# Moving input-panel products ahead of five mixer steps in a hybrid decoder layer: five numbers in a hand-written TensorE order

## The chip, the cores and the metric

The kernel runs on one core of one Trainium2 chip. The metric is the device time of one execution in microseconds (us); the shown time is the median of three runs. Five engines work side by side, each through its own list of instructions: TensorE (PE in the profile, with PEld for its weight loads), VectorE (DVE), ScalarE (ACT), GpSimd (POOL) and SyncE (SP), which here issues the loads. An instruction that needs another engine's result waits at the head of its engine's list, and everything behind it on that engine waits too.

## The reference, cut to what matters

One layer over 256 tokens of width 2048, all in float32. The layer normalizes `x`, multiplies it with `w_in`, feeds one half of the result to a causal pooling mixer and the other to an RWKV-7 time mixer with 16 heads of 64, multiplies both outputs with `w_out`, and goes on with a squared-ReLU MLP and a gated embedding.

```python
h = rms_norm(x, attn_norm[i])
z = h @ w_in[0]
z_pool = z[..., :POOL_WIDTH]
zs = token_shift(z[..., POOL_WIDTH:IN_WIDTH], mu_shift[i])
pool_out = ...            # windowed means of z_pool, times pool_w, times pool_scale
# rwkv7_time_mix of zs = [r, k, v, w, a, g], per head and step t:
#   w, a, g come from narrow inputs through small matrices (low rank)
#   kk = k * k_k, normalized;  k = k * (1 + (a - 1) * k_a)
sa = einsum('bhij,bhj->bhi', S, a_t)
S = S * w_t + sa * b_t + v_t * k_t
y = einsum('bhij,bhj->bhi', S, r_t)
# y is normalized per head;  y += sum(r * k * r_k) * v   (the bonus);  y *= g
mix = concatenate([pool_out, rwkv_out])
x = x + mix @ w_out[i]
x = x + square(relu(rms_norm(x) @ w_ffn_up[i])) @ w_ffn_down[i]
x = x + sigmoid(rms_norm(x) @ w_ple_gate[i]) * (p[i] @ w_ple_proj[i])
return rms_norm(x, final_norm)
```

## The kernel before

**Panels.** A weight matrix is loaded in panels of 128 x 1024 (`raw_...`, 512 KB each, issued by SP). Each panel is split for exactness into a high part `wh` (two copies on ACT, L167) and a rest `wl` (one subtraction on DVE, L168). A panel holds two contraction blocks of 128 rows for 512 columns, and there are two tiles of 128 tokens; PE multiplies each block and token tile with the high part twice (the activations' high part at L241, their rest at L242) and then with the rest once (L238). So a panel is eight products with `wh`, taken in four yields of two, and four with `wl`, taken in four yields of one. Three buffers each hold `raw`, `wh` and `wl`, so panel number i takes the buffers of panel i-3: its `raw` is free when the `wl` of that panel is computed, its `wh` and `wl` when PE has multiplied with them. SP issues the loads in order, so a load that waits for its buffer holds up those behind it.

**The queue.** The panel products of the mixer are generators that stand in a list `queue`: `zk0`, `zr0`, `zv0` (key, receptance and value inputs of heads 0 to 7), `zk1`, `zr1` (heads 8 to 15), `zp0` (pooling), `zv1`, `zp1`, and then the output products `o0a` to `o3a`. PE's order is written out by hand: ahead of a mixer step stands a call that takes products out of the queue. `steps(n)` takes n yields, `fill(us)` takes yields until their declared costs (0.45 for two products with `wh`, 0.23 for one with `wl`) reach the number, and `finish(gen)` takes all that is left up to the end of one generator. A larger number moves panel products ahead of a step; the queue is then shorter later on, and the shift ends at the next `finish`. `z_product` ends with `finish`, `fill(us)` and the transposes `zkT`, `zrT` or `zvT` of its result (L498).

**The other engines.** Each yield also advances `pace`, which puts DVE steps of the triangular inverse (`X`, L724 and L728) in between. Up to the end of the low-rank step `wag_out` the orders of DVE and ACT are fixed as written; behind it a scheduler orders DVE and ACT by priority, and it sees the new order of PE too.

**The steps that are touched.**
- *Head and low-rank transposes.* `head` ends with four sums of squares (`sbank`, L441) and `steps(1)`. ACT takes their root (`rs_n`, L450), DVE the reciprocal (L451), ACT scales the low-rank result (`wagS`, two halves, L459), and PE transposes it (`wagT`, L464 and L465).
- *Second key transposes.* ACT scales the finished banks of `zk1` (`zk1s`, L488); PE transposes (`zkT`); ACT and DVE mix each token with its predecessor (`zk_t`, L335 and L336); ACT squares it (`tF_t`, L585); PE sums the squares per head (`kkn`, L595).
- *Bonus sums.* `rwkv_values` multiplies the values (`vt`) and forms the bonus sums (`bsum`, L523) in the two banks that the receptance transposes `zrT` held until DVE read them (L336).
- *State steps.* `rwkv_core` goes over four chunks c of 64 tokens: ACT copies the right-hand side (`R`, L818), PE multiplies (`um`, L854), ACT copies (`UV`, L858), PE forms the state update (`sm`, L863). The values are due in this form for the first eight heads (gi = 0) and the second (gi = 1).

Of the kernel before, what the change touches and what calls it, by code (L numbers as in the profile page):

```python
# [40 lines left out]
def trunk(  # L41
# [32 lines left out]
    def rw_bank(name):  # L74
        return psr.tile([128, 512], F32, tag="rw", name=name)
# [192 lines left out]
    def fill(us):  # L268

        while us > 0 and queue:  # L270
            us -= advance()

    def steps(n):
        for _ in range(n):
            advance()
# [126 lines left out]
    def head():  # L402
        load_xT(0, 1)
        load_wag("tE", 0, 1)
        load_xT(1, 1)
        load_wag("tF", 1, 1)
        ready(8)
        wag_prod(0, 1)
        wag_prod(1, 1)
        steps(8)  # L410
        load_xT(2, 2)
        load_wag("zr", 2, 2)
        load_xT(4, 4)
        load_wag("zv", 4, 2)
        wag_prod(2, 2)
        wag_prod(4, 2)
        steps(8)
        sums.append(squares(0))
        load_wag("BK", 6, 2)
        load_xT(8, 4)  # L420
        load_wag("BKt", 8, 2)
        wag_prod(6, 2)
        wag_prod(8, 2)
        steps(8)
        sums.append(squares(1))
        load_wag("zk", 10, 2)
        load_xT(12, 4)
        load_wag("tE", 12, 2)
        wag_prod(10, 2)
        wag_prod(12, 2)  # L430
        steps(8)
        sums.append(squares(2))
        load_wag("tF", 14, 2)
        wag_prod(14, 2)
        steps(10)
        sums.append(squares(3))
        steps(3)
        derived()
        for tt in range(2):
            for i, q in enumerate((1, 3)):  # L440
                nc.tensor.matmul(  # L441
                    sbank[:, tt : tt + 1], sums[q][:, 0, tt * 128 : (tt + 1) * 128], ones[:, 0:1],
                    start=i == 0 and tt == 0, stop=i == 1, skip_group_check=True,
                )
        steps(1)

    rs1 = const.tile([128, 2], F32, tag="rs", bufs=2, name="rs_n1")

# [324 lines left out]
    def rwkv_values(gi, st, zv):  # L773

        uvs = [rp.tile([128, 2, 8, 64], F32, tag=f"q{i}", name=f"UV{gi}_{i}") for i in range(2)]
        UV = [uvs[c // 2][:, c % 2] for c in range(4)]
        for tt in range(2):
            b = rw_bank("vt")
            for p in range(4):
                nc.tensor.matmul(b[:, p * 128 : (p + 1) * 128], zv[:, p, tt * 128 : (tt + 1) * 128], cen, start=True, stop=True)  # L780
            for i in range(2):
                with tc.high_priority(30000):
                    nc.scalar.activation(flat3(UV[2 * tt + i])[64:128], b[i * 64 : (i + 1) * 64, :], AF.Copy)
        bon = st["rk"]
        bf, vf = flat(bon), flat(zv)
        block_sum(
            st["rk"], f"rk{gi}",
            lambda hf, b: nc.vector.tensor_tensor(
                bf[:, hf * 512 : (hf + 1) * 512], b, vf[:, hf * 512 : (hf + 1) * 512], op=ALU.mult
            ),  # L790
        )
        st["UV"] = UV

    def rwkv_core(gi, st):
# [34 lines left out]
        for c in range(4):  # L829
# [11 lines left out]
            if 0 < c < 3:  # L841
                for e in range(2):
                    r = slice(e * 64, e * 64 + 64)
                    with tc.high_priority(30000):
                        nc.vector.tensor_tensor(
                            nxt[r, :, r], cur[r, :, r], pc[r, :, c : c + 1].to_broadcast([64, 4, 64]), op=ALU.mult
                        )
            fill(1.59 if gi else 1.14)
            ub = rw_bank("um")
            if c < 3:  # L850
                sb = rw_bank("sm")
# [4 lines left out]
                    direct(b_next, c + 1, h)  # L856
            with tc.high_priority(30000):
                nc.scalar.activation(flat3(UV[c])[0:64], ub[0:64, :], AF.Copy)  # L858
            fill(0.72 if gi else 0.86)
            if c < 3:  # L860
                for h in range(8):
                    e, p = h % 2, h // 2
# [33 lines left out]
    def flat3(t_):  # L896
        return t_.rearrange("s h i -> s (h i)")
# [109 lines left out]
    z_zk1 = z_product(4, "zk", "mu_k", 1)  # L1007
# [20 lines left out]
    zv0 = z_zv0()  # L1028
    fill(0.25)
    st1 = rwkv_lora(1)  # L1030
    rwkv_k(1, st1, z_zk1(1.33))
    rwkv_r(1, st1, z_zr1())
    run(beside.pop(0) if beside else ())
    beside.clear()
# [455 lines left out]
```

## Time and profile before

| what | value |
|---|---|
| median of 3 runs | 1180.49 us (1180.44 to 1181.11) |
| the profiled execution | 1180.25 us, its span 1178.2 us |
| granted TensorE clock | 0.998 of full speed |
| DVE, ACT busy | 873.3 us (74%), 709.3 us (60%) |
| HBM | 183 GB/s over the span |

The mixer, in which all five places lie, takes the first part of the span, up to about 345 us; the MLP's products `u_w` and the rest follow. A timeline row gives start, duration, engine, source line, operation and tile names (`out<-in`), the number of instructions in the row, and in brackets the idle time of the engine ahead of it with the releaser. Durations of matmuls overlap, so the distance from one start to the next says how fast PE goes. A table of windows gives the busy time of every engine in a stretch.

### The profile page before, as it was taken

Reading aid. Unit: us, or ns where it says so; the run is one execution under the profiler, and the core shown is the slowest. Engines: PE = TensorE matmul, PEld = TensorE weight load, DVE = VectorE, ACT = ScalarE, POOL = GpSimd, SP = SyncE. Lnnn points to the kernel's source line nnn. Section 1 sums busy time; section 2 is a strip of 40 time slices with the busy share of each in tenths; the row PEclk is TensorE's granted clock in tenths of the full one; section 3 lists DMA queues with packets and bytes.
Section 4 is the critical chain, followed back from the end, with each engine's and each line's share of the span. In section 5 each row is a group of like instructions: output and inputs, shape, how many; then the busy total and the mean of one; then the engine's idle time right before and its main releaser. Section 6 shows DMA issues by size and latency. Waiting matters only on the chain.

```text
span 1178.2 us, 17287 instructions
## 1 busy us (share of the span) xinstructions
PE 1162.5 (99%) x6419; PEld 973.4 (83%) x6419; DVE 873.3 (74%) x1188; ACT 709.3 (60%) x1309; POOL 13.7 (1%) x73
## 2 busy tenths in 40 slices
PE   8999999999999999999999999999999999999997
PEld 8787777788887888888888888888888888888886
DVE  7786996964656666767988987676668879788543
ACT  7776848676545565555665664555556655568543
POOL 2100000000000000000000000000000000000000
PEclk9999999999999999999999999999999999999999
DMA  7464343354465555555556556555555555767511
GB/s 290 154 202 146 135 140 119 119 179 157 160 203 178 177 182 196 184 192 200 187 204 212 198 202 209 186 191 191 185 195 190 202 205 195 290 233 249 197 56 72
DMA packets 60756, 216.81 MB, mean 184 GB/s; under 512 B 6784, under 2 KB 7552, under 8 KB 60288
## 3 DMA queue, kind: packets, MB, share of 16 engines
q1 hardware_dynamic: 60240, 214.99, 52.5%
q8 instruction: 50, 0.82, 0.3%
q10 hardware_dynamic: 432, 0.73, 0.2%
q14 instruction: 34, 0.28, 0.1%
HBM read 213.59 MB, written 2.10 MB: 183 GB/s over the span
## 4 chain that ended last, share of the span: by engine, by line
PE 96%; ACT 1%; DVE 1%; DMA 0%; issue 0%; SPq 0%; POOL 0%; DVEq 0%; POOLq 0%
PE u_w L1112 20%; PE u_w L1117 10%; PE d_b L1231 7%; PE d_b L1229 7%; PE d_b L1230 7%; PE d_w L1231 2%; PE d_w L1229 2%; PE d_w L1230 2%; PE gt_b L242 2%; PE gt_b L241 2%; PE gt_b L238 2%; PE zk_b L241 1%; PE zk_b L242 1%; PE o_b L241 1%; PE o_b L242 1%; PE zv_b L238 1%
## 5 line engine op out<-in xcount | busy, mean ns | idle before, releaser
L1112 PE MATMUL u_w<-h,wh_u 128*128 128x512 f32 x1024 | 321.9, 395 | 0.0
L167 ACT ACTIVATE wh_u<-raw_u 128x512 fp32r<-128x512 f32 x256 | 147.5, 623 | 160.9 <-issue 98.2
L168 DVE TENSOR_TENSOR wl_u<-raw_u,wh_u 128x1024 fp32r<-128x1024 f32 x128 | 156.6, 1224 | 105.2 <-ACT wh_u L167 103.5
L1117 PEld LDWEIGHTS u_w<-h,wl_u 128*128 128x128 f32 x1024 | 192.4, 188 | 45.4
L1117 PE MATMUL u_w<-h,wl_u 128*128 128x256 f32 x1024 | 201.4, 278 | 0.0
L1112 PEld LDWEIGHTS u_w<-h,wh_u 128*128 128x128 f32 x1024 | 156.0, 189 | 0.1
L168 DVE TENSOR_TENSOR wl_gt<-raw_gt,wh_gt 128x1024 fp32r<-128x1024 f32 x24 | 29.4, 1224 | 23.2 <-ACT wh_gt L167 23.2
L167 ACT ACTIVATE wh_gt<-raw_gt 128x512 fp32r<-128x512 f32 x48 | 28.0, 638 | 23.1 <-PE gt_b L242 14.4
L241 PE MATMUL gt_b<-wh_gt,h 128*128 128x512 f32 x96 | 37.3, 389 | 0.0
L242 PE MATMUL gt_b<-wh_gt,h 128*128 128x512 f32 x96 | 37.3, 389 | 0.0
L168 DVE TENSOR_TENSOR wl_o<-raw_o,wh_o 128x1024 fp32r<-128x1024 f32 x16 | 19.6, 1222 | 12.9 <-ACT wh_o L167 9.9
L167 ACT ACTIVATE wh_o<-raw_o 128x512 fp32r<-128x512 f32 x32 | 18.4, 623 | 16.3 <-issue 8.5
L167 ACT ACTIVATE wh_zp<-raw_zp 128x512 fp32r<-128x512 f32 x32 | 18.6, 623 | 15.7 <-PE zp_b L242 7.2
L168 DVE TENSOR_TENSOR wl_zk<-raw_zk,wh_zk 128x1024 fp32r<-128x1024 f32 x16 | 19.4, 1220 | 10.4 <-ACT wh_zk L167 10.4
L241 PE MATMUL zk_b<-wh_zk,hTh 128*128 128x512 f32 x64 | 25.2, 394 | 1.4 <-ACT wh_zk L167 1.4
L241 PE MATMUL zv_b<-wh_zv,hTh 128*128 128x512 f32 x64 | 26.0, 406 | 0.0
L167 ACT ACTIVATE wh_zk<-raw_zk 128x512 fp32r<-128x512 f32 x32 | 18.4, 622 | 12.4 <-PE zv_b L242 4.0
L241 PE MATMUL zp_b<-wh_zp,hTh 128*128 128x512 f32 x64 | 25.7, 401 | 0.0
L238 PE MATMUL gt_b<-wl_gt,h 128*128 128x512 f32 x96 | 25.7, 389 | 0.0
L168 DVE TENSOR_TENSOR wl_zv<-raw_zv,wh_zv 128x1024 fp32r<-128x1024 f32 x16 | 19.4, 1218 | 8.2 <-ACT wh_zv L167 7.4
L241 PE MATMUL zr_b<-wh_zr,hTh 128*128 128x512 f32 x64 | 25.4, 397 | 0.0
L242 PE MATMUL zp_b<-wh_zp,hTl 128*128 128x512 f32 x64 | 25.0, 391 | 0.0
(840 smaller groups left out, 2963.9 us busy)
## 6 DMA issues: line engine op xcount, KB each, us to landing
raw_u<-in_w_ffn_up_dram SPq DMA_DIRECT2D x128, 512.0 KB, 3.5
raw_d<-in_w_ffn_down_dram SPq DMA_DIRECT2D x128, 512.0 KB, 4.3
raw_gt<-in_w_ple_gate_dram SPq DMA_DIRECT2D x24, 512.0 KB, 3.5
raw_zk<-in_w_in_dram SPq DMA_DIRECT2D x16, 512.0 KB, 3.7
raw_zr<-in_w_in_dram SPq DMA_DIRECT2D x16, 512.0 KB, 3.3
raw_zv<-in_w_in_dram SPq DMA_DIRECT2D x16, 512.0 KB, 3.3
raw_zp<-in_w_in_dram SPq DMA_DIRECT2D x16, 512.0 KB, 3.2
raw_o<-in_w_out_dram SPq DMA_DIRECT2D x16, 512.0 KB, 4.2
```

What stands on the lines that cost most here:

```text
L167: nc.scalar.activation(wh[:, a * 512 : (a + 1) * 512], raw[:, a * 512 : (a + 1) * 512], AF.Copy)
L168: nc.vector.tensor_tensor(wl, raw, wh.bitcast(F32), op=ALU.subtract)
L238: nc.tensor.matmul(banks[tt], ah[:, ts_], halves[a][1], start=False, stop=last)
L241: nc.tensor.matmul(banks[tt], ah[:, ts_], halves[a][0], start=i + a == 0, stop=False)
L242: nc.tensor.matmul(banks[tt], al[:, ts_], halves[a][0], start=False, stop=False)
L1112: nc.tensor.matmul(bank[:, ct, :].rearrange("p (s t) -> p s t", s=2), wh[:, cs[ct]], hl, start=k == 0, stop=False, skip_group_check=True,)
L1117: nc.tensor.matmul(bank[:, ct, 0:T], wl[:, cs[ct]], hl[:, 0, :], start=False, stop=k == 15, skip_group_check=True)
L1229: nc.tensor.matmul(banks[n], ah, wh, start=first, stop=False)
L1230: nc.tensor.matmul(banks[n], ah, wl, start=False, stop=False)
L1231: nc.tensor.matmul(banks[n], al, wh, start=False, stop=last)
```

## The change

Five numbers change, and no instruction is added or left out. Ahead of the low-rank transposes six more yields are taken (`steps(7)` for `steps(1)`: two more products with `wl` of panel five of `zk0`, and the eight with `wh` of panel six). Ahead of the second key transposes `fill` rises from 1.33 to 1.90, which is three products. Ahead of the first bonus sums a new `fill(0.92)` takes six products. In the first state step of the first heads the fill ahead of `um` rises from 1.14 to 1.59 and that ahead of `sm` from 0.86 to 1.76, three products each. In `fill(0.00 ...)` nothing is taken. From L784 on, lines of the changed kernel have a number one higher.

```diff
--- before.py
+++ after.py
@@ -442,7 +442,7 @@
                     sbank[:, tt : tt + 1], sums[q][:, 0, tt * 128 : (tt + 1) * 128], ones[:, 0:1],
                     start=i == 0 and tt == 0, stop=i == 1, skip_group_check=True,
                 )
-        steps(1)
+        steps(7)
 
     rs1 = const.tile([128, 2], F32, tag="rs", bufs=2, name="rs_n1")
 
@@ -781,6 +781,7 @@
             for i in range(2):
                 with tc.high_priority(30000):
                     nc.scalar.activation(flat3(UV[2 * tt + i])[64:128], b[i * 64 : (i + 1) * 64, :], AF.Copy)
+        fill(0.00 if gi else 0.92)
         bon = st["rk"]
         bf, vf = flat(bon), flat(zv)
         block_sum(
@@ -845,7 +846,7 @@
                         nc.vector.tensor_tensor(
                             nxt[r, :, r], cur[r, :, r], pc[r, :, c : c + 1].to_broadcast([64, 4, 64]), op=ALU.mult
                         )
-            fill(1.59 if gi else 1.14)
+            fill(1.59 if gi or c == 0 else 1.14)
             ub = rw_bank("um")
             if c < 3:
                 sb = rw_bank("sm")
@@ -856,7 +857,7 @@
                     direct(b_next, c + 1, h)
             with tc.high_priority(30000):
                 nc.scalar.activation(flat3(UV[c])[0:64], ub[0:64, :], AF.Copy)
-            fill(0.72 if gi else 0.86)
+            fill(0.72 if gi else 0.86 if c else 1.76)
             if c < 3:
                 for h in range(8):
                     e, p = h % 2, h // 2
@@ -1028,7 +1029,7 @@
     zv0 = z_zv0()
     fill(0.25)
     st1 = rwkv_lora(1)
-    rwkv_k(1, st1, z_zk1(1.33))
+    rwkv_k(1, st1, z_zk1(1.90))
     rwkv_r(1, st1, z_zr1())
     run(beside.pop(0) if beside else ())
     beside.clear()
```

Since the queue is shared, the orders of ACT and DVE change along with PE's. At the low-rank step, ACT (the rows from the root of the sums on; `wagS` is the scaled low-rank result, `wh_zr` a split receptance panel) has before:

```order
L450 ACTIVATE rs_n_175<-sbank,eps_n 128x2
L459 ACTIVATE wagS<-wag_b_169,rs_n_175 128x288
L459 ACTIVATE wagS<-wag_b_170,rs_n_175 128x288
L335 ACTIVATE zf<-wagT,omu 128x256
L471 ACT_TABLE_LOAD
```

and now:

```order
L450 ACTIVATE rs_n_175<-sbank,eps_n 128x2
L459 ACTIVATE wagS<-wag_b_169,rs_n_175 128x288
L167 ACTIVATE wh_zr_1_622<-raw_zr_1_620 128x512 x2
L459 ACTIVATE wagS<-wag_b_170,rs_n_175 128x288
L335 ACTIVATE zf<-wagT,omu 128x256
```

The split of receptance panel one has moved in between the two halves of `wagS`. At the same place DVE has, before, the last key panel's rest directly ahead of the reciprocal:

```order
L144 TENSOR_SCALAR oka<-par_sb 128x8
L145 SCALAR_TENSOR_TENSOR cen<-jsum,ident 128x128
L168 TENSOR_TENSOR wl_zk_7_561<-raw_zk_7_558,wh_zk_7_560 128x1024
L451 RECIPROCAL rs_n_175<-rs_n_175 128x2
L133 TENSOR_TENSOR wband<-wband,ident 128x128
```

and now:

```order
L168 TENSOR_TENSOR wl_zk_6_518<-raw_zk_6_515,wh_zk_6_517 128x1024
L168 TENSOR_TENSOR wl_zk_7_561<-raw_zk_7_558,wh_zk_7_560 128x1024
L168 TENSOR_TENSOR wl_zr_0_585<-raw_zr_0_582,wh_zr_0_584 128x1024
L451 RECIPROCAL rs_n_175<-rs_n_175 128x2
L133 TENSOR_TENSOR wband<-wband,ident 128x128 x2
```

The rest of receptance panel zero, `wl_zr_0`, has moved ahead of the reciprocal. At the second key transposes, DVE (`zk_t` is the token mix behind `zkT`, `X` the inverse) has before:

```order
L724 TENSOR_TENSOR X_1131<-X_1131,AT_1130 128x120
L728 TENSOR_TENSOR X_1131<-X_1131 128x10x12
L724 TENSOR_TENSOR X_1131<-X_1131,AT_1130 128x121
L336 SCALAR_TENSOR_TENSOR zk_t<-zkT_1350,par_sb,zk_t 128x255
L728 TENSOR_TENSOR X_1131<-X_1131 128x11x11
L336 SCALAR_TENSOR_TENSOR zk_t<-zkT_1351,par_sb,zk_t 128x255
L724 TENSOR_TENSOR X_1131<-X_1131,AT_1130 128x110
L728 TENSOR_TENSOR X_1131<-X_1131 128x11x10
L336 SCALAR_TENSOR_TENSOR zk_t<-zkT_1350,par_sb,zk_t 128x255
L724 TENSOR_TENSOR X_1131<-X_1131,AT_1130 128x108
L336 SCALAR_TENSOR_TENSOR zk_t<-zkT_1351,par_sb,zk_t 128x255
```

and now:

```order
L724 TENSOR_TENSOR X_1131<-X_1131,AT_1130 128x120
L728 TENSOR_TENSOR X_1131<-X_1131 128x10x12
L724 TENSOR_TENSOR X_1131<-X_1131,AT_1130 128x121
L728 TENSOR_TENSOR X_1131<-X_1131 128x11x11
L724 TENSOR_TENSOR X_1131<-X_1131,AT_1130 128x110
L728 TENSOR_TENSOR X_1131<-X_1131 128x11x10
L724 TENSOR_TENSOR X_1131<-X_1131,AT_1130 128x108
L336 SCALAR_TENSOR_TENSOR zk_t<-zkT_1355,par_sb,zk_t 128x255
L336 SCALAR_TENSOR_TENSOR zk_t<-zkT_1356,par_sb,zk_t 128x255
L168 TENSOR_TENSOR wl_zr_3_1446<-raw_zr_3_1443,wh_zr_3_1445 128x1024
L336 SCALAR_TENSOR_TENSOR zk_t<-zkT_1355,par_sb,zk_t 128x255
L336 SCALAR_TENSOR_TENSOR zk_t<-zkT_1356,par_sb,zk_t 128x255
```

Four more steps of the inverse stand ahead of the first `zk_t`, and the rest `wl_zr_3` stands between the second and the third. At the first state step ACT (`wh_zv` is a split value panel, `tmp` belongs to the inverse's use, `UV` follows `um`) has before:

```order
L950 ACTIVATE zt_1942<-zp_b_1585,rs_n_175 128x512
L167 ACTIVATE wh_zv_2_2073<-raw_zv_2_2071 128x512
L818 ACTIVATE R_1966<-rym 64x2x128 x2
L167 ACTIVATE wh_zv_2_2073<-raw_zv_2_2071 128x512
L167 ACTIVATE wh_zv_3_2149<-raw_zv_3_2147 128x512 x2
L710 ACTIVATE tmp_1927<-tmp_1927 64x1024
L858 ACTIVATE UV_0_1655<-um 64x512
```

and now:

```order
L764 ACTIVATE SC_950<-qm 32x8x32 x4
L951 ACTIVATE zt_1929<-zp_b_1585,rs_n_175 128x512
L167 ACTIVATE wh_zv_3_2088<-raw_zv_3_2086 128x512
L819 ACTIVATE R_1981<-rym 64x2x128 x2
L167 ACTIVATE wh_zv_3_2088<-raw_zv_3_2086 128x512
L709 ACTIVATE tmp_1945<-SC_1773 32x1024
L167 ACTIVATE wh_zv_4_2174<-raw_zv_4_2172 128x512 x2
L710 ACTIVATE tmp_1945<-tmp_1945 64x1024
L859 ACTIVATE UV_0_1655<-um 64x512
```

Between `R` and `UV` a piece of `tmp` (L709), which stood ahead of `R` before, has been added; a half panel, a whole panel and L710 stand there in both.

## Prediction

> **What bounds the kernel now.** I read the page first: busy times and the chain that ended last.
>
> ```profile
> span 1178.2 us, 17287 instructions
> PE 1162.5 (99%) x6419; PEld 973.4 (83%) x6419; DVE 873.3 (74%) x1188; ACT 709.3 (60%) x1309; POOL 13.7 (1%) x73
> PE 96%; ACT 1%; DVE 1%; DMA 0%; issue 0%; SPq 0%; POOL 0%; DVEq 0%; POOLq 0%
> ```
>
> PE is the bound: 1162.5 of 1178.2 us busy, 96% of the chain. The change takes no work from PE, so it can win only PE's idle time, 15.7 us at most, and of that only what lies at the five places. The waits of PE, grouped, come next (us, times, longest).
>
> ```profile
> PE bsum L523 <- DVE zr_t L336: 1.0, 1, 1.0
> PE sm L863 <- ACT UV L858: 0.9, 1, 0.9
> PE wagT L464 <- POOL wband L130: 0.8, 1, 0.8
> PE zkT L498 <- ACT zk1s L488: 0.8, 2, 0.6
> PE um L854 <- ACT R L818: 0.4, 1, 0.4
> ```
>
> The five edits stand exactly ahead of these five waits: 1.0 + 0.9 + 0.8 + 0.8 + 0.4 = 3.9 us. But a busy PE need not be a fast one, so I read the windows for what surrounds these waits (busy us and count by engine, granted clock, DMA share, GB/s).
>
> ```profile
> 130.00:160.00 30.00, 28.90 (x142) 22.69 (x140) 29.34 (x57) 21.29 (x41) 0.78 (x3) 1.00 0.52 175
> 250.00:345.00 95.00, 95.00 (x720) 77.81 (x719) 52.93 (x70) 54.27 (x111) 0.96 (x2) 1.00 0.50 169
> ```
>
> From 130 to 160 us DVE is busy 29.34 of 30 us: whatever is put ahead of a DVE step there delays it in full. From 250 to 345 us PE has no idle time, so a lag or a lead gained earlier passes to the end unchanged.
>
> **Edit 1, low-rank transposes.** PE first, then ACT and DVE, around the place.
>
> ```profile
> 36.78 0.48 PE L238 MATMUL zk_b<-wl_zk,hTh 128*128 128x512 f32 x1
> 38.11 0.41 PE L464 MATMUL wagT<-ident,wagS 128*128 128x128 f32 x2 [0.85 <-POOL wband L130]
> 39.95 0.39 PE L242 MATMUL zk_b<-wh_zk,hTl 128*128 128x512 f32 x1
> 41.08 1.07 PE L238 MATMUL zk_b<-wl_zk,hTh 128*128 128x512 f32 x4
> 35.93 1.15 ACT L167 ACTIVATE wh_zr<-raw_zr 128x512 fp32r<-128x512 f32 x2 [0.89 <-PE zk_b L242]
> 37.47 0.89 ACT L459 ACTIVATE wagS<-wag_b,rs_n 128x288 f32<-128x288 f32 x2 [0.23 <-DVE rs_n L451]
> 37.26 0.17 DVE L451 RECIPROCAL rs_n<-rs_n 128x2 f32<-128x2 f32 x1 [0.96 <-ACT rs_n L450]
> 41.74 1.21 DVE L168 TENSOR_TENSOR wl_zr<-raw_zr,wh_zr 128x1024 fp32r<-128x1024 f32 x1
> ```
>
> Five products start from 39.95 to 41.08, 0.227 us each. Ten more ahead of the transposes are 2.3 us; the demand moves from 37.26 to about 39.5, past the 38.11 at which the transposes now start. So far the 0.85 us is gone. But in the new order DVE makes `wl_zr_0` ahead of the reciprocal, and that needs the buffer that PE frees with its last `wl` product of panel five. Two more products behind 36.78 (0.48 long) end at about 37.6; with 1.21 us for `wl_zr_0` the reciprocal starts at 38.9 instead of 37.26, and the first half of `wagS` ends near 39.6. Behind it ACT has `wh_zr_1`, which needs the `wh` buffer of panel six, free when PE ends its eight products, near 39.5; it takes 1.15 us, so the second half ends at about 41.2. The second group of transposes waits for it, and the next product starts near 41.4 where it stood at 41.08 before. I take +0.3 us. The ends: −0.85 (all of the wait goes) and +0.9 (ACT late by half a `wh_zr_1` more). `wl_zr_0` itself was hidden in idle time of DVE; its cover is gone, and the reciprocal pays for it.
>
> **Edit 2, second key transposes.** The two waits of PE, and the ACT step they wait for.
>
> ```profile
> 128.60 0.33 PE L498 MATMUL zkT<-ident,zk1s 128*128 128x128 f32 x1 [0.56 <-ACT zk1s L488]
> 129.18 0.98 PE L498 MATMUL zkT<-ident,zk1s 128*128 128x128 f32 x7 [0.25 <-ACT zk1s L488]
> 127.88 1.24 ACT L488 ACTIVATE zk1s<-zk_b,rs_n 128x512 f32<-128x512 f32 x2
> ```
>
> ACT ends `zk1s` at 129.12, and its order up to there stays. Three more products are 0.68 us, and they fit into the gap of 0.56 + 0.25 = 0.81: I take −0.7, with 0 and −0.8 as ends.
>
> **What follows on edit 2: the head sums `kkn`.** These are eight products behind a fixed fill, and no wait is listed for them. Compare the first group (58.06) with the second (134.64).
>
> ```profile
> 58.06 0.64 PE L595 MATMUL kkn<-tF_t,jhead 128*32 128x256 f32 x8
> 58.63 0.50 PE L241 MATMUL zr_b<-wh_zr,hTh 128*128 128x512 f32 x1
> 134.64 2.13 PE L595 MATMUL kkn<-tF_t,jhead 128*32 128x256 f32 x8
> 136.70 0.50 PE L241 MATMUL zr_b<-wh_zr,hTh 128*128 128x512 f32 x1
> 134.55:136.70 2.15, 2.06 (x10) 0.55 (x9) 2.01 (x9) 1.92 (x6) 0.00 (x0) 1.00 0.05 21
> 132.81 0.47 DVE L336 SCALAR_TENSOR_TENSOR zk_t<-zkT,par_sb,zk_t 128x255 f32<-128x255 f32 x1
> 134.85 0.47 DVE L336 SCALAR_TENSOR_TENSOR zk_t<-zkT,par_sb,zk_t 128x255 f32<-128x255 f32 x1
> 135.54 0.26 DVE L724 TENSOR_TENSOR X<-X,AT 128x96 f32<-128x96 f32 x1
> 135.83 0.26 DVE L728 TENSOR_TENSOR X<-X 128x96 f32<-128x96 f32 x1
> 134.79 1.30 ACT L585 ACTIVATE tF_t<-zk_t,par_sb 128x256 f32<-128x256 f32 x3 [0.23 <-DVE zk_t L336]
> ```
>
> The same eight take 0.57 us to the next start there and 2.06 here: a hidden wait of 1.5 us, which the row of the window shows as PE busy. It is for `tF_t`, and so for the DVE steps `zk_t`. In the new order four more steps of the inverse stand ahead of the first `zk_t` (4 x 0.29, the distance from 135.54 to 135.83: 1.16 us), and `wl_zr_3` (1.21, less the steps that leave) between the second and third. DVE has no slack to hide them. The four start at about 134.0, 134.4, 135.9 and 136.3 instead of 132.81 to 134.85; ACT, with a half panel between its last two squares, ends near 137.9 instead of 136.1; the next product starts near 138.6, not 136.70. Two of the three added products (0.45 us) are still ahead at `kkn`, the fills counting whole yields, so PE reaches it at about 134.4, 0.2 earlier than before since it won 0.7 at `zkT`. The hidden wait is then 138.6 − 134.4 − 0.57, about 3.6 us instead of 1.5: +2.1, of which I take 2.0, the times being read to a tenth. Ends: −0.4 (the order does not matter and the 0.45 covers part of the old wait) and +2.1.
>
> The Trainium skill, Perfetto Trace Analysis, section Identifying the Most-Contended Engine, says that matmul busy time is a poor measure for TensorE and to look at the weight loads' busy time instead. The trace agrees, and it decides the sum: in the window above PE is busy 2.06 us and its weight loads only 0.55. By the busy row `kkn` has nothing to lose and the change would give about 2 us; by the weight loads it is the costliest term.
>
> **Edit 3, bonus sums.**
>
> ```profile
> 159.49 1.96 PE L523 MATMUL bsum<-ybuf,jsum 128*128 128x512 f32 x4 [1.01 <-DVE zr_t L336]
> 159.66 0.48 DVE L336 SCALAR_TENSOR_TENSOR zr_t<-zrT,par_sb,zr_t 128x255 f32<-128x255 f32 x1
> ```
>
> PE asks at 158.5 and DVE frees the first bank before the last read at 159.66. Six more products (1.37 us) move the demand to 159.85, and PE's lag of about 1.6 us from before to 161.5, by which the last reading has ended even if it is one us late. So the 1.01 us is gone and pays back part of `kkn`: −1.0, with 0 as the other end.
>
> **Edits 4 and 5, first state step.**
>
> ```profile
> 196.57 0.69 PE L863 MATMUL sm<-UV,BKt 128*64 128x64 f32 x16 [0.88 <-ACT UV L858]
> 194.85 1.06 ACT L710 ACTIVATE tmp<-tmp 64x1024 f32<-64x1024 f32 x1
> ```
>
> `um` is asked for 2.5 us later in PE's order and `R` moves less: −0.4 (ends 0, −0.4). Between `R` and `UV` ACT now also has L709, priced by its neighbour L710 at 1.06. The six products of the two fills put `sm` 0.7 later against `um`; 0.88 + 1.06 − 0.7 = 1.2 would be left if all came together, 0.2 if `R` is early by one us. I take 0.6 left, −0.3 (ends −0.9, +0.3).
>
> **The sum.** 0.3 − 0.7 + 2.0 − 1.0 − 0.4 − 0.3 = −0.1 us, on 1180.25 of the profiled execution: 1180.2. The profiled run lies 0.24 under the median of the three, 1180.49. A change under 0.2%, 2.4 us, cannot be told from none by this measurement: under 1178.1 is faster, over 1182.9 slower.
>
> **The rivals.** (a) All five waits go and nothing takes their place: 1180.25 − 3.9 = 1176.3. For it: each edit stands ahead of a listed wait. Against it: the order of DVE at `kkn`, and the half of `wagS` behind `wh_zr_1`.
>
> (b) The order of the inverse steps does not matter, so `kkn` stays at 1.5 us hidden: 0.3 − 0.7 − 1.0 − 0.4 − 0.3 = −2.1, or 1178.1, and 1177.6 with `sm`'s other half. It is decided by where DVE starts the last `zk_t`: at 135.0 or before.
>
> (c) Slower: the ACT order in the second heads' inverse. With the queue shorter by up to 2.73 us of products, the second output panel's split now stands on ACT ahead of the pooling's `mp` and the inverse's `T1G`.
>
> ```profile
> 251.63 0.47 ACT L996 ACTIVATE mp<-pm,par_sb 128x256 fp32r<-128x256 f32 x1 [0.69 <-PE pm L182]
> 254.59 1.55 ACT L764 ACTIVATE T1G<-gm 32x256 f32<-32x256 f32 x4
> 258.83 1.15 PE L757 MATMUL qm<-SC,T1G 32*64 32x64 f32 x32
> 247.55 9.12 SPq L158 DMA_DIRECT2D raw_o0a<-in_w_out_dram  x3
> DMA to landing us min/median/max: 4.9/6.5/8.1
> ```
>
> `T1G` ends 2.7 us ahead of `qm` (256.14 to 258.83); the fill in between loses six products, 1.36, so 1.3 are left. The load of `x` (landing row, 4.9 to 8.1 us) now stands ahead of the first output panel on SP. If the second panel, issued at 247.55 and later by the shift of 2.73, lands only after 8.1 us, at 258.4, it misses `mp` (254.4, less 1.15 for its split, plus 1.3 of slack: 254.6) by 3.8: 1180.2 + 3.8 = 1184.0. Decisive is a landing behind about 257.3, 2.7 late; SP issued it at 247.55 with time to spare, against it.
>
> (d) The waits only move, each edit giving back what it takes: 1180.25, inside the forecast.
>
> **How the numbers follow.** The forecast with (d), from 1178.6 to 1182.0, 0.60; (b) 0.22; (a) 0.08; (c) 0.10. Under 1178.1 lie (a) and over half of (b), 0.22; over 1182.9 most of (c), 0.09; between them 0.69. The range must reach into (b) and the low part of (c): 1177.3 to 1182.6; left out are (a) and the upper part of (c), and some of (b) at its edge, about 2 in 10.
>
> **What would show it.** Right: `wagT` in two groups with a wait for ACT `wagS` between them, next product near 41.4; `zkT` without a wait over 0.2; `kkn` of eight lasting about 4 us, DVE's `zk_t` from about 134; no wait at `bsum` or `um`; about 0.6 at `sm`; `qm` without a wait. The forecast is wrong if `kkn` lasts no longer than 2.1, or if PE waits anywhere between 250 and 345 us.

## The result, and the profile after

The changed kernel takes 1185.55 us (median of 6, 1183.62 to 1188.28) where the kernel before takes 1180.47 on the same chip: ratio 1.0042, interval 1.0029 to 1.0054. It is slower by 5.1 us; the forecast was no change, 1180.2, and the time lies outside its range. Three of the runs below had one execution each of 1448 to 1846 us at a granted clock of 0.59 to 0.75; all times and ratios leave these out, and a ratio is an estimate from all other executions, not the quotient of two medians. The profiled execution, 1183.62 us, is the fastest of the six, 3.4 us longer than the profiled one of before. So two things have to be explained: 3.4 us that this trace shows, and about 2 us that it does not.

The page of the changed kernel: span, busy times, and the chain that ended last.

```profile
span 1181.6 us, 17290 instructions
PE 1163.5 (98%) x6419; PEld 973.8 (82%) x6419; DVE 873.8 (74%) x1188; ACT 708.7 (60%) x1309; POOL 16.1 (1%) x73
PE 94%; ACT 2%; DVE 2%; DMA 1%; issue 0%; SPq 0%; DVEq 0%; ACTq 0%
```

The work is the same; PE's share of the chain falls from 96 to 94%, and ACT and DVE have 2% each. The waits of PE (us, times, longest):

```profile
PE kkn L595 <- ACT tF_t L585: 2.4, 3, 1.1
PE sc L669 <- ACT UV L783: 1.6, 1, 1.6
PE sm L864 <- ACT UV L859: 1.3, 1, 1.3
PE wagT L464 <- ACT wagS L459: 0.9, 1, 0.9
PE qm L757 <- ACT T1G L764: 0.4, 1, 0.4
PE wagT L464 <- POOL wband L130: 0.3, 1, 0.3
PE rym L835 <- DVE sbd L875: 0.3, 1, 0.3
PE zkT L498 <- ACT zk1s L488: 0.2, 1, 0.2
PE um L855 <- ACT R L819: 0.2, 1, 0.2
```

Three waits at the five places are nearly gone (`zkT` 0.8 to 0.2, `bsum` 1.0 to none, `um` 0.4 to 0.2). The two at the top are new: `kkn`, which was foreseen, and the second heads' scores `sc`, which the forecast did not have. The windows of after, and the second one of before beside it (busy us and count by engine, granted clock, DMA share, GB/s):

```profile
130.00:160.00 30.00, 27.65 (x138) 21.99 (x138) 28.95 (x54) 20.10 (x40) 0.77 (x3) 1.00 0.50 175
160.00:190.00 30.00, 28.45 (x216) 21.95 (x214) 22.55 (x30) 16.44 (x34) 1.27 (x2) 1.00 0.37 124
250.00:345.00 95.00, 94.50 (x717) 76.98 (x717) 53.12 (x72) 55.42 (x116) 0.96 (x2) 1.00 0.49 174
```

```profile
160.00:190.00 30.00, 30.00 (x225) 23.53 (x224) 22.31 (x29) 19.17 (x38) 1.08 (x2) 1.00 0.36 124
```

From 160 to 190 us PE was always busy before and issued 225 products; now it idles for 1.55 us and issues 216.

**The lag, step by step.** For each step I take its start after minus its start before, less 0.227 us for every product that now stands ahead of it. That is how far PE is behind its old self; only where it changes does a step cost or win.

| step | predicted | measured |
|---|---|---|
| start of the execution up to the first panel | – | −1.2 |
| `wagT` | +0.3 | +0.55 |
| `zkT` | −0.7 | −0.65 |
| `kkn` | +2.0 | +2.2 |
| second receptance sums and transposes | 0 | −0.15 |
| `bsum` | −1.0 | −1.2 |
| scores of the second heads | 0 | +2.0 |
| `um` | −0.4 | −0.5 |
| `sm` | −0.3 | +0.2 |
| third state chunk (`sbd`) | 0 | +1.1 |
| from `qm` to the second heads' values | 0 | +0.7 |
| the rest, up to the MLP | 0 | +0.5 |
| sum (rows rounded) | −0.1 | +3.4 |

The first row is not of the change: the order up to there is the same, and the first key panel was landed and split 1.2 us earlier in this execution. All other profiles of this case lead that of the kernel before at the head's sums too, by 0.0 to 1.2 us, so that one was a late start. The change's own rows add up to 4.6 us. The steps that were listed sum to about +0.55 instead of −0.1; what the list left out is about +4.1. The last row was not followed further.

### The profile page after: what moved, and what is told of

It reads as the page before. It is cut to its first block, busy times and chain, and to the rows that moved or that the text cites. A ratio compares the mean times of both kernels' runs of the same rounds, so it can differ in the third digit from the quotient of the medians.

```text
span 1181.6 us, 17290 instructions
## 1 busy us (share of the span) xinstructions
PE 1163.5 (98%) x6419; PEld 973.8 (82%) x6419; DVE 873.8 (74%) x1188; ACT 708.7 (60%) x1309; POOL 16.1 (1%) x73
## 4 chain that ended last, share of the span: by engine, by line
PE 94%; ACT 2%; DVE 2%; DMA 1%; issue 0%; SPq 0%; DVEq 0%; ACTq 0%
PE u_w L1113 20%; PE u_w L1118 10%; PE d_b L1231 7%; PE d_b L1230 7%; PE d_b L1232 7%; PE d_w L1230 2%; PE d_w L1231 2%; PE d_w L1232 2%; PE gt_b L241 2%; PE gt_b L242 2%; PE gt_b L238 2%; PE o_b L241 1%; PE o_b L242 1%; PE zk_b L238 1%; PE o_b L238 1%; PE zk_b L241 1%
```

## The experiments

**Each part alone.** `steps(7)` alone:

```diff
-        steps(1)
+        steps(7)
```

> Only the head edit (steps(7)). Theory A, each edit brings the waits that its own reordering makes: the second half of the low-rank transposes waits about 0.9 us for the scaled half behind the split of receptance panel one, the reciprocal stands behind one more rest; lag behind the transposes +0.3 to +0.5 against before, nothing later: the time +0.3 to +0.5. Theory B, the shown wait simply goes: -0.8. Theory C, the shortened queue costs later: 0, since its shift ends at the key transposes.

1180.08 us against 1180.7, ratio 0.9995 (0.9986 to 1.0003): no change that can be told. The lag behind `wagT` is 0.0 and stays within 0.1 through the mixer; since this execution led by 0.55 us ahead of it, the place costs 0.55, as in the whole change. Kernels with the old order lose 0 to 0.5 us of such a lead there as well, so the edit's own price is not clear. The wait of 0.8 is now one of 0.3 and one of 0.9. The key part alone:

```diff
-    rwkv_k(1, st1, z_zk1(1.33))
+    rwkv_k(1, st1, z_zk1(1.90))
```

> Only the fill ahead of the second key transposes (1.90). Theory A: the transposes gain 0.7, the head sums kkn lose 2.1 (four more inverse steps and one rest ahead on DVE), the bonus sums then find their bank free and give back 1.0: +0.4 in all. Theory B: -0.7 to -0.8. Theory C: 0, the shift ends at the receptance transposes.

1181.87, ratio 1.0015 (1.0006 to 1.0024). Steps: `zkT` −0.7, `kkn` +2.2, the receptance transposes −0.2, `bsum` −0.6, scores +0.5: net +1.25. The forecast's price for `kkn` is confirmed by itself, and the wait at `bsum`, as was expected, took back only a part. The bonus part alone:

```diff
+        fill(0.00 if gi else 0.92)
         bon = st["rk"]
```

> Only the new fill ahead of the bonus sums (0.92). Theory A: the bonus sums gain 1.0, the second pair of score banks waits for ACT's copy out of the second value bank (in before the third pair did) and loses 1.9 to 2.0, the first state update loses some 0.3 to 0.5 more since L709 stands ahead of its copy on ACT: +1.2 to +2.5 with what follows. Theory B: -1.0. Theory C: +0.5 to +1.5, lost late, where the queue runs out, and nothing at the scores.

1185.42, ratio 1.0041 (1.0029 to 1.0054): as much as the whole change, from the part that was to win 1.0. It does win 1.2 at `bsum`; then the second score pair loses 4.1, of which 2.1 are waits (1.7 and 0.4); the rest is explained last. The state part alone:

```diff
-            fill(1.59 if gi else 1.14)
+            fill(1.59 if gi or c == 0 else 1.14)
-            fill(0.72 if gi else 0.86)
+            fill(0.72 if gi else 0.86 if c else 1.76)
```

> Only the two fills of the first state step. The orders of ACT, DVE and the banks stay as before up to there. Theory A: the waits of um (0.4) and sm (0.9) go, -1.0 to -1.3 at the place, and at most 0.3 back later. Theory B: the same, -1.3. Theory C: +0.5 to +1.5 where the queue is shorter later on.

1182.1, ratio 1.0009 (1.0000 to 1.0018). `sm` wins 1.35, the third chunk loses 2.0. And the whole change without the bonus part:

```diff
-        fill(0.00 if gi else 0.92)
```

> The whole change without the fill ahead of the bonus sums. Theory A, the single runs add up (head -0.6, key transposes +1.2, state fills +1.4): +1 to +2 against before, and no wait of the scores for ACT's copy of the values. Rival, the loss comes from the four edits acting together: about as slow as the whole change, +4 to +5.

1182.69, ratio 1.0020 (1.0010 to 1.0029). The parts add up: about −0.6 + 1.2 + 1.4. So the bonus fill costs most, and the rest is `kkn` and the third chunk.

**Why the bonus fill costs: a PSUM bank.** The score pairs before (PE, then ACT):

```profile
173.83 1.26 PE L669 MATMUL sc<-AR,BK 64*128 64x128 f32 x16
177.96 1.16 PE L669 MATMUL sc<-AR,BK 64*128 64x128 f32 x16
172.83 2.13 ACT L743 ACTIVATE SC<-X 32x1024 f32<-32x1024 f32 x2 [1.96 <-DVE X L739]
175.40 1.20 ACT L783 ACTIVATE UV<-vt 64x512 f32<-64x512 f32 x2
```

and after:

```profile
174.91 0.48 PE L669 MATMUL sc<-AR,BK 64*128 64x128 f32 x2
176.95 1.16 PE L669 MATMUL sc<-AR,BK 64*128 64x128 f32 x14 [1.55 <-ACT UV L783]
175.70 1.19 ACT L783 ACTIVATE UV<-vt 64x512 f32<-64x512 f32 x2
```

The step `vt` wrote the values of the first heads into a bank long before. ACT copies them to `UV` only at 175.4, since `UV` has the SBUF buffer of the inverse and must wait until L743 has read `X` out of it. Till then the bank is held. Four banks go round among the mixer steps, each to the next step that asks when it is free. Which step has which bank is read from the order and the waits here, not from a row of its own. Before, the pair at 173.83 got two other banks and the pair at 177.96 this one, free at 176.6. With the bonus fill the banks change hands in another order, and the pair at 174.91 gets it: PE issues two products into the first bank and stands until the copy has ended. To test this I gave `UV` of the first heads another SBUF buffer, so that its copy need not wait for `X`; first without any fill:

```diff
-        uvs = [rp.tile([128, 2, 8, 64], F32, tag=f"q{i}", name=f"UV{gi}_{i}") for i in range(2)]
+        if gi:
+            uvs = [...]            # as before
+        else:
+            uv = a8(0, "UV0").rearrange("p (b a h i) -> p b a h i", b=2, a=2, h=8)
+            uvs = [uv[:, i] for i in range(2)]
```

> Before, with the values' copy UV of the first heads in a buffer of its own (a slot that stands empty then) and no fill changed: a control for the next run. ACT copies them at about 158 us instead of 175 and 188, and all four banks are free by then. Theory A: no wait of before lies on these banks, so 0 within 0.5; the bonus sums still wait about 1.0.

1180.83, ratio 1.0003 (0.9994 to 1.0012): the buffer alone changes nothing that can be told. With it and the bonus fill:

> Only the fill ahead of the bonus sums (0.92), with UV in its own buffer as in the run before. Theory A, the slowness of that fill (+4.7) is the bank that the second pair of scores shares with the uncopied values: the wait at the scores (3.7 to 4.1 us) goes and the gain of 1.0 at the bonus sums stays: -0.5 to +0.7 against before. Rival, it is the shorter queue or the order on DVE: it stays at +3 to +5.

```profile
173.87 1.16 PE L669 MATMUL sc<-AR,BK 64*128 64x128 f32 x16
```

1181.25, ratio 0.9999 (0.9990 to 1.0008), and no wait is listed at the scores. So the 5 us of the bonus fill hang on the bank: the wait, and the half clock behind it that is told below. But the win at `bsum` doesn't reach the end either: the lag, −0.5 ahead of the place, is −1.8 at `sm` of the second chunk and −0.6 at the third. With the whole change:

> The whole change with UV in its own buffer. Theory A: of its +5.0 the wait of the scores for the bank (1.96 in its trace) goes and the rest (kkn 2.2, the later chunks 1.1) stays: +2 to +3.5 against before. Rival, the bank is all of it, since the fill alone cost 4.7: 0 to +1.

1184.56, ratio 1.0036 (1.0023 to 1.0049). No wait at the scores, and no gain that can be told (the whole change had 1.0042, and 1.0036 when it ran again): now the third chunk waits for DVE.

```profile
212.97 0.38 PE L839 MATMUL rym<-sbd,AR 128*128 128x128 f32 x1 [2.18 <-DVE sbd L879]
213.00:217.00 4.00, 4.00 (x14) 3.28 (x14) 3.23 (x9) 0.95 (x3) 0.00 (x0) 0.57 0.39 131
```

The bank was the cause in the bonus fill alone; in the whole change its removal uncovers the next one. The second row, a window, is taken up below: its granted clock is 0.57.

**Moving the head sums later.** The key part, with more products ahead of `kkn`:

```diff
+    rwkv_k(1, st1, z_zk1(1.90))
-        fill(4.19 if gi else 5.06)
+        fill(6.47 if gi else 5.06)
```

> The key transposes' fill at 1.90, and ten more products (fill 6.47 for 4.19 in the second heads) ahead of the head sums kkn, so that PE comes there after DVE. Theory D, DVE sets the time from 110 to 160 us: the listed and hidden waits at kkn go (3.6 us), but PE then waits so much longer at the bonus sums for DVE's last reading of the receptance banks (2 to 3.5 us in place of 0.4): -0.3 to +0.5 against before in all. Rival, PE sets it and the wait at kkn is a plain loss: -1.5 to -2.2.

1186.31, ratio 1.0042 (1.0029 to 1.0054): a miss, and worse than the part without it. At `kkn` the added 2.2 us are gone: the eight products take 1.96 us to the next start, so the wait is about 1.4, as in the kernel before. But a wait has moved to `bsum` and is longer:

```profile
161.03 3.75 PE L523 MATMUL bsum<-ybuf,jsum 128*128 128x512 f32 x4 [3.27 <-DVE AR L638]
```

The products ahead of `kkn` brought no VectorE time: what hangs on `kkn` comes later by them (DVE's `AR` of L638 starts at 160.78, before at 157.15).

**Why the wins don't last: DVE.** Third-chunk rows, before (DVE), then the state part alone (DVE, PE):

```profile
205.98 0.86 DVE L874 TENSOR_TENSOR sbd<-sbd,sm 64x256 f32<-64x256 f32 x2
207.78 1.23 DVE L168 TENSOR_TENSOR wl_zv<-raw_zv,wh_zv 128x1024 fp32r<-128x1024 f32 x1
```

```profile
208.08 1.22 DVE L168 TENSOR_TENSOR wl_zv<-raw_zv,wh_zv 128x1024 fp32r<-128x1024 f32 x1
209.41 0.86 DVE L874 TENSOR_TENSOR sbd<-sbd,sm 64x256 f32<-64x256 f32 x2
210.32 0.49 PE L834 MATMUL rym<-sbd,AR 128*128 128x128 f32 x2 [1.18 <-DVE sbd L874]
```

Before, DVE added the state update (`sbd`) and then made the next panel's rest; now the panel comes first, because PE, being ahead with its products, has freed the buffer earlier. PE waits 1.18 us for `sbd`. Would the win stay if the queue were brought back to its old length right behind the step? Three kernels: bonus fill, then six products fewer ahead of the scores; state fills, then as many fewer at the end of the first chunk; and both with `steps(7)`.

```diff
-    fill(8.39)
+    fill(7.02)
-                fill(1.07 if gi else 1.61)
+                fill(1.07 if gi else 1.61 if c else 0.26)
```

> The fill ahead of the bonus sums (0.92), and as many products less behind them (8.39 becomes 7.02 ahead of the scores), so that the queue is as before from the scores on. Theory E, what costs is that all later steps come later against the panels (orders of ACT and DVE, banks), not the place itself: the orders are then those of before but for two rests, the third pair of scores meets the bank as before, and the gain of 1.0 stays: -1.0 to -0.5 against before. Rival, the place costs: +3 to +5 as in the run with the fill alone.

> The two fills of the first state step, and six products less behind it (1.61 becomes 0.26 ahead of the second chunk's reading of the state). Theory E: the waits of um and sm go (1.1 to 1.3), the wait of rym for the state at the third chunk (1.2) does not come: -1.2 to -0.8 against before. Rival: rym waits at the second chunk instead, since its cover is taken: 0.

> The head edit, the bonus sums and the first state step together, the last two given back as in the two runs before, the key transposes as in the kernel before. Theory E, by the single runs: -0.6 - 1.0 - 1.2 = -2.8, or 1177.8 to 1178.5. Rival: the gains at the bonus sums are taken back at the next wait for DVE or ACT: -0.6 to -1.5.

1181.11, 1181.05 and 1181.14 against 1181.0: ratios 1.0003 (0.9994 to 1.0012), 1.0002 (0.9993 to 1.0011) and 1.0000 (0.9991 to 1.0009). All the losses are gone, and so are the wins. The first wins 1.2 at `bsum` and gives it back at the next two score pairs; the second wins 1.36 at `sm` and gives it back at the third chunk. PE in the first, then DVE and PE in the second:

```profile
175.03 1.20 PE L669 MATMUL sc<-AR,BK 64*128 64x128 f32 x8 [0.72 <-DVE SC L676]
```

```profile
205.55 0.86 DVE L874 TENSOR_TENSOR sbd<-sbd,sm 64x256 f32<-64x256 f32 x2
206.47 0.49 PE L834 MATMUL rym<-sbd,AR 128*128 128x128 f32 x2 [1.04 <-DVE sbd L874]
```

`sbd` starts at 205.55 where it started at 205.98 before; this execution was 0.47 ahead already from the start. So DVE is as late as ever, and PE, 1.36 earlier, waits 1.04 for it. In the kernel before, DVE is full or nearly so in both stretches (windows of 170 to 176 and of 196 to 206 us; the third pair of numbers is DVE's):

```profile
170.00:176.00 6.00, 6.00 (x48) 4.85 (x47) 5.99 (x8) 3.98 (x6) 0.00 (x0) 1.00 0.24 89
196.00:206.00 10.00, 9.43 (x125) 7.82 (x126) 9.18 (x28) 7.26 (x15) 0.00 (x0) 1.00 0.47 159
```

At the two places tested the wait was not PE's to win: behind it stands DVE's own queue, and a PE that comes earlier waits at the next step.

If that is so, a shorter DVE queue should turn the sign. In three more kernels the inverse stops after 8 of its 31 pairs of steps (the other 23 are left out): the kernel before, the whole change, and the change with both shifts given back but without the key part.

```diff
-        for k in range(31):
+        for k in range(8):
```

> A control: before, with the triangular inverse's DVE steps cut from 31 to 8 pairs in both groups (this part of the computation is left out), so that DVE has slack from 110 to 178 us and beside the state steps. Theory D, DVE's backlog sets the time at kkn, the bonus sums and the state's reading: the hidden 1.5 us at kkn and most of the 1.0 at the bonus sums go, the waits for ACT (zk1s 0.8, UV 0.9, R 0.4) and at the head 0.85 stay: -1.5 to -2.5 against before. Rival, PE's order sets it: 0.

> The whole change, with the same 23 of 31 pairs of the inverse's steps left out. Theory D: with DVE's backlog gone and the bank free earlier (the copy of the values waits for the inverse's end), the losses at kkn, at the scores and at the third chunk go, and the waits for ACT that the edits cover go as well: faster than the control by 0.5 to 2.5 us, where the whole change lost 5.0 with the full inverse. Rival, the moved products cost by themselves (shorter queue, order of ACT): 3 to 5 us slower than the control.

> Head edit, bonus sums and first state step, the last two given back behind the step, with the same part of the inverse left out. Theory D: where the full inverse took all gains back (0.0 against before), they now stay: faster than the control by 1 to 2.5 us. Rival: 0.

1187.4, 1186.0 and 1184.77 against 1180.89: ratios 1.0057 (1.0045 to 1.0070), 1.0040 (1.0028 to 1.0053) and 1.0033 (1.0022 to 1.0044). Against the cut kernel, the change now saves 1.4 and the version given back 2.6, where with the full inverse they cost 5 and 0. That agrees with DVE as the taker, but does not show it, since the control itself missed: with less DVE work it is 6.5 us slower. Two waits are new in it, 2.5 us at `sm` and this one:

```profile
131.07 0.33 PE L498 MATMUL zkT<-ident,zk1s 128*128 128x128 f32 x1 [3.17 <-ACT zk1s L488]
```

The scheduler orders ACT and DVE anew when the inverse is shorter: ACT has waited 1.94 us for DVE (`tB_t`), and a piece of `SC` (L743) with half panels now stands ahead of `zk1s`. The short inverse was not tried with the old order kept. Half of the 6.5 us is the clock of which the next part speaks: 3.4 us in the profile of each of the three. From the first heads' `zvT` to the second heads' values their lag grows by 6.8, 5.4 and 4.5 us, so in these profiles the differences, 1.4 and 2.4, are of waits. In the medians some of them may be clock, since the control's executions have 0.993 to 0.995 and the others 0.995 to 0.998.

**The part that the trace of after does not show: the clock.** In several profiles the windows have a granted clock under 1.00 right behind a long wait. In the trace's record of the clock it is 0.50 for 3.41 us, or for 6.83 us, twice that (from 159.8 to 166.6 us; the wait of 3.27 at `bsum` shown above lasts to 161.03), on a grid of 3.41 us that starts anywhere in an execution. Products stand 0.43 us apart there instead of 0.227. It hits where PE was idle for most of one such window. I laid this grid over all twenty profiles. Behind every window with PE busy for at most 1.53 of 3.41 us the clock fell (26, of which 15 lie at the very end); behind a window at full clock with over 2.3 it never did, and between these in 4 of 32. One fall costs half of 3.41, 1.7 us, and whether a wait of 1.5 us causes it depends on how it lies on the grid. The profile of after has none, so the 2 us by which it is under its median could be this. To tell clock from wait, I took the bonus fill alone and gave PE something to multiply in its wait at the second score pair, eight products whose result is overwritten; beside it the bonus fill and the whole change once more.

```diff
                 for e in range(2):
+                    for _ in range(8 if e and p == 0 and c == 1 and gi == 1 else 0):
+                        nc.tensor.matmul(
+                            bks[0][:, 128:512], hT_h[0][:, 0:128], hT_h[0][:, 0:384],
+                            start=True, stop=True, skip_group_check=True,
+                        )
```

> Only the bonus fill, and in the wait that it brings at the second score pair TensorE multiplies something else: eight products of 128x384 into the part of the first score bank that is overwritten behind them (their results are thrown away; 8 x 0.17 = 1.4 us, less than the 1.7 us of the wait). Orders of VectorE and ScalarE are those of the bonus fill alone. Theory C (new, from the clock records: when TensorE is idle for over half of a 3.41 us window the granted clock is 0.50 in the next one, which costs half of 3.41 = 1.7 us): the wait stays and the lag from it, but the clock stays at 1.00 through 174 to 182 us: 1.7 us less than the same edit without the products, 1183.7, and the granted clock 0.998 or 0.999 in most runs. Rival D (the clock plays no part; order and waits alone): as without the products, 1185.4, with clocks of 0.995 to 0.996 as there. Rival E (the products are in the way): later than 1185.4.

> The bonus fill alone once more, beside the run with the array kept busy. Theory C: 1185.4 as the first time, slower by 1.7 than with the products, with a clock of 0.50 for 3.41 us behind the wait at the scores in most runs (sliding the window over the first profile of this edit, TensorE is under 1.7 us busy in some window in about half of all phases; 5 of the 5 runs had 0.995 to 0.996). Rival D: 1185.4 as well, and the run with the products the same.

> The whole change once more, for its granted clocks run by run: the first six runs fell in three groups, 1183.6 and 1183.8 at 0.998, 1185.5 to 1186.1 (three) at 0.997, 1188.3 at 0.996. Theory C: the groups are none, one and two windows of 3.41 us at half clock (1.7 us each, about 2 with what they delay), so the times stand again near 1183.7, 1185.7 and 1188, falling with the granted clock, and a profile with a clock under 0.998 shows the half clock right behind the head sums (about 135 to 142 us) or the second score pair (about 177 to 181). Rival D: times that do not follow the granted clock, median 1185.5.

With the products 1183.08, ratio 1.0021 (1.0012 to 1.0030); without 1185.11, ratio 1.0038 (1.0024 to 1.0052), beside 1180.9. The stop is as long in both (2.18 and 2.17 us from the pair's first row to its second), and the difference is 2.0 us, about the price of one fall. Windows of the bonus fill alone (its first profile), then of the same with the array busy, with PE's row there:

```profile
174.00:177.00 3.00, 0.91 (x8) 0.72 (x10) 0.94 (x2) 2.93 (x6) 0.00 (x0) 1.00 0.53 175
177.00:181.00 4.00, 4.00 (x20) 3.21 (x17) 2.42 (x3) 3.58 (x10) 0.00 (x0) 0.57 0.12 27
```

```profile
174.00:177.00 3.00, 2.77 (x13) 2.04 (x12) 2.33 (x4) 2.81 (x4) 0.00 (x0) 1.00 0.43 145
177.00:181.00 4.00, 3.92 (x28) 3.13 (x28) 1.30 (x2) 3.96 (x11) 0.00 (x0) 1.00 0.17 69
176.20 1.68 PE L670 MATMUL sc<-hTh 128*128 128x384 f32 x8
```

In the first, 0.91 us of work in 3 us are followed by a clock of 0.57 over four us and 20 products; in the second the clock stays at 1.00 and PE issues 28. This pair of profiles decides nothing by itself: the second profile without the products has no fall at the scores either (its window of the grid holds 1.85 us of work), and both it and the profile with the products have one near 38 us. What counts are the executions: without the products all ten, of both runs, have a mean granted clock of 0.995 to 0.997; with them six of ten have 0.998. The two intervals overlap, so the difference in time rests on these clocks. The products themselves cost nothing that the trace shows, since they fit into the wait.

The whole change, once more: 1185.17, ratio 1.0036 (1.0023 to 1.0049). Its profile, now of a slower execution (1186.62 us), has the half clock at the scores:

```profile
177.20 1.88 PE L669 MATMUL sc<-AR,BK 64*128 64x128 f32 x14 [1.53 <-ACT UV L783]
177.00:181.00 4.00, 3.80 (x19) 3.20 (x20) 2.42 (x3) 3.35 (x10) 0.00 (x0) 0.57 0.13 36
```

Of its 11 executions, four have a mean granted clock of 0.998 and a median of 1183.7; seven have 0.996 or 0.997 and a median of 1186.05. The expectation had these as groups of none, one and two falls; 1185.17 at 0.998 doesn't fit it, the rest does. Of the kernel before, 63 of 107 executions have 0.998 or 0.999 (median 1180.26) and 44 less (1181.7). So in executions without a fall the change costs 1183.7 − 1180.3 = 3.4 us, and the rest of the 5.1, 1.7 us, goes with the falls: 7 of 11 executions now lie below 0.998, and 44 of 107 did before. That the lag table has 3.4 as well is in part chance, since its sum holds the 1.2 us of the early start.

## Why the prediction was wrong

- **`wagT`**, +0.3: right in form, two groups with a wait for `wagS` between them. It measured +0.55 in this trace and alone, of which up to 0.5 can be the lead that the old order loses there too.

```profile
38.58 0.41 PE L464 MATMUL wagT<-ident,wagS 128*128 128x128 f32 x2 [0.26 <-POOL wband L130]
40.00 0.44 PE L464 MATMUL wagT<-ident,wagS 128*128 128x128 f32 x2 [0.90 <-ACT wagS L459]
40.30 1.17 PE L238 MATMUL zk_b<-wl_zk,hTh 128*128 128x512 f32 x4
37.94 0.50 ACT L459 ACTIVATE wagS<-wag_b,rs_n 128x288 f32<-128x288 f32 x1 [1.78 <-DVE rs_n L451]
38.41 1.15 ACT L167 ACTIVATE wh_zr<-raw_zr 128x512 fp32r<-128x512 f32 x2
```

The next product comes at 40.30, which with the 1.16 us by which this execution was early is 41.46; 41.4 was forecast. Between the halves of `wagS` stands the panel's split of 1.15 us.

- **`zkT`**, −0.7: right, −0.65; 0.2 of wait is left.
- **`kkn`**, +2.0: right, +2.2, and +2.2 in the key part alone. Rival (b), that the inverse's order doesn't matter, is refuted. The eight products, now in three pieces with their waits shown, and DVE:

```profile
134.86 0.62 PE L595 MATMUL kkn<-tF_t,jhead 128*32 128x256 f32 x2 [1.00 <-ACT tF_t L585]
136.54 0.63 PE L595 MATMUL kkn<-tF_t,jhead 128*32 128x256 f32 x4 [1.06 <-ACT tF_t L585]
137.46 0.62 PE L595 MATMUL kkn<-tF_t,jhead 128*32 128x256 f32 x2 [0.29 <-ACT tF_t L585]
138.01 0.50 PE L241 MATMUL zr_b<-wh_zr,hTh 128*128 128x512 f32 x1
133.43 0.86 DVE L336 SCALAR_TENSOR_TENSOR zk_t<-zkT,par_sb,zk_t 128x255 f32<-128x255 f32 x2
134.21 1.22 DVE L168 TENSOR_TENSOR wl_zr<-raw_zr,wh_zr 128x1024 fp32r<-128x1024 f32 x1
135.34 0.87 DVE L336 SCALAR_TENSOR_TENSOR zk_t<-zkT,par_sb,zk_t 128x255 f32<-128x255 f32 x2
```

PE asks at 133.86 and goes on at 138.01: 4.15 us, of which 0.57 are work, so 3.6 of wait, the forecast's number. Reading the weight loads instead of the busy time was decisive.
- **`bsum`**, −1.0, and **`um`**, −0.4: right, −1.2 and −0.5; neither waits over 0.2. **`sm`**, −0.3: wrong in size, +0.2; 1.3 of wait is left, the upper of the two values that were weighed.
- **The step that failed is the sum.** It took the five places and `kkn` for all that the change touches, and held that elsewhere a lag passes on unchanged. But the change also moved DVE's and ACT's panel work and the banks behind those places. The scores (+2.0, a bank), the third chunk (+1.1, DVE behind a panel) and 1.2 later on stood in no term. Of the four rivals none had it. Rival (c) had the right side, and gave 1184.0. Its mechanism is there, but small: the second output panel's split does stand ahead of `mp` and `T1G`, and `qm` waits 0.4 us for `T1G` (lag +0.7) where 3.8 were priced; in the second profiled execution of the change, where ACT waited for the first output panel's landing, it waits 1.3 (lag +1.7). By this wait, in the stretch from 250 to 345 us that was taken to be free of waits, one of the forecast's own signs of being wrong came true. The second panel's split on ACT in the first profile, then the first panel's in the second:

```profile
257.46 1.14 ACT L167 ACTIVATE wh_o0a<-raw_o0a 128x512 fp32r<-128x512 f32 x2
```

```profile
257.55 1.15 ACT L167 ACTIVATE wh_o0a<-raw_o0a 128x512 fp32r<-128x512 f32 x2 [3.51 <-DMA raw_o0a<-in_w_out_dram]
```

- **The second miss is the clock.** The rows that the prediction quoted all had 1.00, and it priced each wait at its own length. The new waits at `kkn` and at the scores can make the clock fall behind them, at 1.7 us: at the scores by the window shown, at `kkn` at 138.2 us in the profile of the whole change with `UV` in its own buffer. 7 of 11 executions have a mean clock that says so, though not at which of the two. The Trainium skill, TensorE: Matmul & The Clock Gate, section Part 1: The HAM clock gate (the "warmup" mystery), describes this: a free-running window of 3413 ns and half the clock after an idle one. The trace agrees in the window (3.41 us) and in the half; but the section asks for an idle window, and section HAM oscillation — how this bites in real kernels speaks of gaps over about 3.4 us, whereas here a gap of 1.5 us was enough (the scores in the second profile of the change: a wait of 1.53 us, PE busy 1.88 in that window).
- **Rival (d)**, that the waits only move, held for the wins: each of the three kernels that gave the shift back ended at the time before. It failed in the price, since in the change as written the waits also grew.

No version here beats the kernel before by more than the noise.

## What to carry to other kernels

A number that moves products ahead of a waiting step also frees panel buffers and banks earlier for everything behind it: after such an edit, compare for each engine what now stands ahead of the operands of the next few steps, and which step now gets a bank that is released late. A short wait that goes is no gain where the next steps wait for an engine that is full in that stretch: at the two places tested, PE came earlier and waited there. What is left to try is less work on the full engine, or another order there; no run here shows such a gain cleanly. And price a wait of about 1.5 us or more on TensorE with the half clock that may follow it, from the granted clock of several executions, as one profile can lack it.

## What the runs showed of the hardware

- The granted clock fell to 0.50 for 3.41 or 6.83 us behind every window of 3.41 us in which TensorE worked for 1.53 us or less; between 1.53 and 2.3 us it fell in 4 of 32. One fall is 1.7 us by its length; measured were 2.0 (1185.11 against 1183.08, without and with the products in the wait) and 1.5 (1184.2 against 1182.7, the executions with the products below 0.998 and at it; likewise 1181.7 against 1180.3 for the kernel before).
- Eight useless products of 1.7 us in a stop of 2.2 us did not lengthen it (2.18 against 2.17 us), and the runs with them are 2.0 us shorter.
- Five profiles of kernels that keep the old order up to there have such a fall near 38 us, where `wagT` waits for 1.4 to 1.9 us (0.85 in the profile of the kernel before, which has none). That the kernel before has it in its 44 executions below 0.998, and that this is part of their spread from 1179.3 to 1183.6, is likely but not shown. With `steps(7)` alone 10 of 11 executions have a clock of 0.998 or more, against 63 of 107; the gain of 0.6 us that this would give is within the interval of that run.
